# A chunk scan of a state-space branch: from a doubling scan on two engines to a tree on one, with 128-row output matmuls

## The chip, the cores and the metric

The kernel runs on one core of one Trainium2 chip. The metric is the device time of one execution in microseconds (us). Several executions are made and their median is taken.

## What is computed

Two transformer-like blocks run one after the other on 1024 tokens of width 1024, all in float32. The first holds attention, a state-space (SSM) branch and a convolutional feed-forward; the second holds three gated branches. Only the SSM branch is touched by the change. The reference computes it as a scan over tokens:

```python
def combine(left, right):
    ar1, ai1, xr1, xi1 = left
    ar2, ai2, xr2, xi2 = right
    return (ar2 * ar1 - ai2 * ai1,
            ar2 * ai1 + ai2 * ar1,
            ar2 * xr1 - ai2 * xi1 + xr2,
            ar2 * xi1 + ai2 * xr1 + xi2)

_, _, xr, xi = lax.associative_scan(combine, (a_re_t, a_im_t, bu_re, bu_im), axis=1)
y = (jnp.einsum('bsgn,gcn->bsgc', xr, c_re)
     - jnp.einsum('bsgn,gcn->bsgc', xi, c_im) + d_skip * ug)
```

There are 16 groups of 64 complex states; `a` does not depend on the token.

## The kernel before

All the large products are TensorE matmuls whose operands are split into a high and a low part (`fp32r`), three matmuls for one product. A weight block of 128x1024 comes in by DMA, ScalarE casts its high part and VectorE subtracts to get the low part (`split_to`, lines 608 to 626; this is called a split below). A matmul cannot start before its block is split.

The order of the work is not written by hand. Every operation is recorded in a `Plan` (line 155); `schedule` (lines 293 to 444) plays the recorded program with a cost for each operation and with a limit on the live buffers (`NSLOT` = 50 of 128x1024, kinds of them with limits of their own), and `issue` hands the instructions to the engines in the order that results. So every instruction has the line 450, each engine works off its own fixed list, and a list waits as a whole when its next instruction waits. Buffers have the names `s…`, PSUM tiles `mm…` (two banks) and `tr…` (one bank).

The SSM branch is a generator, `ssm_gen` (line 964). The code that computes the attention and SSM gates (lines 1557 to 1569) takes up to `NSTEP` = 3 steps of it after each gate block. A gate block is one weight block and 48 matmuls of 512 columns in one `mm` tile, and the gate blocks are the work that TensorE has beside the scan. The tokens are cut into 128 chunks of 8. `vr` and `vi` (line 1211) hold for each chunk the state that it adds, real and imaginary part, 128 partitions (two halves of 64 states) by 8 groups by 128 chunks. Lines 1227 to 1247 scan over the 128 chunks in seven doubling levels; at level `l` every chunk from `d = 2**l` on gets a rotated copy of the chunk `d` before it:

```python
pt(q[2], v3r[:, :, 0:w], ai, ALU.mult)      # GpSimd
pt(q[3], v3i[:, :, 0:w], ar, ALU.mult)      # GpSimd
tt(q[0], v3r[:, :, 0:w], ar, ALU.mult)      # VectorE, as the four below
tt(q[1], v3i[:, :, 0:w], ai, ALU.mult)
tt(q[0], q[0], q[1], ALU.subtract)
tt(v3r[:, :, d:], v3r[:, :, d:], q[0], ALU.add)
tt(q[2], q[2], q[3], ALU.add)
tt(v3i[:, :, d:], v3i[:, :, d:], q[2], ALU.add)
```

This is 42 operations on VectorE and 14 on GpSimd. Then (lines 1249 to 1265) 16 groups give their output in one PSUM tile for every four: a matmul of `ut` with `kt` on 128 rows, and one each of `vr` with `car` and of `vi` with `cai` on the 64 rows of the group's half. These are 48 plain float32 matmuls of 128 columns; the profile counts two records for each. They are called the output matmuls below. A gelu follows (`gelu2`, on ScalarE and VectorE), transposes, and a small gated product. The kernel then goes on to the query and key blocks and the attention.

Of the kernel before, what the change touches and what calls it, by code (L numbers as in the profile page):

```python
# [14 lines left out]
AF = mybir.ActivationFunctionType  # L15
ALU = mybir.AluOpType
# [449 lines left out]
def kernel(ctx: ExitStack, tc: tile.TileContext, x, wts, wada, vecs, rows, ssmv, wglu, ttab, iden,  # L466
                           out, dbg=None):
    nc = Plan(tc.nc)
# [15 lines left out]
    def slot(p, dt=F32, group=None):  # L484
        return nc.buffer(dt, group)
# [56 lines left out]
    def mm(ps, l, r, start, stop):  # L542
        nc.tensor.matmul(out=ps, lhsT=l, rhs=r, start=start, stop=stop)

    def act(o, i, f, scale=1.0, bias=0.0, acc=None):
        kw = {}
        if acc is not None:
            kw["accum_out"] = acc
        nc.scalar.activation(out=o, in_=i, func=f, scale=scale, bias=bias, **kw)
# [4 lines left out]
    def tt(o, a, b, op):  # L554
        nc.vector.tensor_tensor(out=o, in0=a, in1=b, op=op)

    def ts(o, a, s1, s2, op0, op1=None):
        if op1 is None:
            nc.vector.tensor_scalar(out=o, in0=a, scalar1=s1, scalar2=None, op0=op0)
        else:  # L560
            nc.vector.tensor_scalar(out=o, in0=a, scalar1=s1, scalar2=s2, op0=op0, op1=op1)
# [402 lines left out]
    def ssm_gen(xs):  # L964
# [83 lines left out]
        z = mul(r, r)  # L1048
        sp = lin(z, -1.9515295891e-4, 8.3321608736e-3)
        sp = mul(sp, z)  # L1050
        q = T()
# [173 lines left out]
            yield  # L1225

        v3r, v3i = (v.rearrange("p (a j) -> p a j", a=8) for v in (vr, vi))
        for l in range(7):
            d = 1 << l
            w = 128 - d  # L1230
            ar = pre(8 + l).rearrange("p (a o) -> p a o", o=1).to_broadcast([128, 8, w])
            ai = pim(8 + l).rearrange("p (a o) -> p a o", o=1).to_broadcast([128, 8, w])
            q = [slot("t").rearrange("p (a j) -> p a j", a=8)[:, :, 0:w] for _ in range(4)]

            def pt(o, x_, y_, op):
                nc.gpsimd.tensor_tensor(out=o, in0=x_, in1=y_, op=op)

            pt(q[2], v3r[:, :, 0:w], ai, ALU.mult)
            pt(q[3], v3i[:, :, 0:w], ar, ALU.mult)
            tt(q[0], v3r[:, :, 0:w], ar, ALU.mult)  # L1240
            tt(q[1], v3i[:, :, 0:w], ai, ALU.mult)
            tt(q[0], q[0], q[1], ALU.subtract)
            yield
            tt(v3r[:, :, d:], v3r[:, :, d:], q[0], ALU.add)
            tt(q[2], q[2], q[3], ALU.add)
            tt(v3i[:, :, d:], v3i[:, :, d:], q[2], ALU.add)
            yield

        yg = [slot("yg"), slot("yg")]
        for gh in range(2):  # L1250
            k3 = kt[gh].rearrange("p (t g c) -> p t g c", t=8, g=8)
            y3 = yg[gh].rearrange("p (t c) -> p t c", t=8)
            for h in range(2):
                ps = tr_ps()
                p3 = ps.rearrange("p (t g c) -> p t g c", t=8, g=4)
                for j in range(4):
                    gl = 4 * h + j
                    pr, b = gl, 64 * gh
                    o = p3[:, :, j, :]
                    mm(o, ut[gh][:, 128 * gl:128 * gl + 128], k3[:, :, gl, :], True, False)  # L1260
                    mm(o, vr[b:b + 64, 128 * pr:128 * pr + 128], car[b:b + 64, 128 * pr:128 * pr + 128], False, False)
                    mm(o, vi[b:b + 64, 128 * pr:128 * pr + 128], cai[b:b + 64, 128 * pr:128 * pr + 128], False, True)
                t = slot("gl")
                gelu2(y3[:, :, 64 * h:64 * h + 64], ps, t, lambda a: a.rearrange("p (t c) -> p t c", t=8))
                yield
# [1134 lines left out]
```

## Time and profile before

| | us |
|---|---|
| median of three runs | 2127.89 |
| the runs | 2118.71, 2127.90, 2127.89 |
| the profiled execution, its own time | 2118.8 |
| its span, first to last instruction | 2116.7 |
| TensorE (PE) busy in it | 2032.1 (96%) |
| VectorE (DVE) busy | 1375.1 (65%) |
| ScalarE (ACT) busy | 748.4 (35%) |
| GpSimd (POOL) busy | 494.9 (23%) |
| mean granted TensorE clock | 0.977 of full speed |

A row of the profile gives engine, operation, output and inputs by name (numbers left out), shape, count and duration. `idle before <-` names what ended an idle time. A count of PE is in records: a `fp32r` matmul of 512 columns is one, a plain float32 matmul two.

### The profile page before, as it was taken

What the parts mean: (1) busy time and instruction counts of PE and PEld (TensorE: products, weight loads), DVE (VectorE), ACT (ScalarE), POOL (GpSimd) and SP (SyncE); (2) the same over time, 40 slices, a digit from 0 to 9 for tenths busy, and PEclk for the clock granted to TensorE, in tenths of its full rate; (3) what the DMA queues carried; (4) which work ended last, traced back from release to release, by engine and by line L of the source; (5) the groups of instructions that cost most, each with busy time, mean ns of one, the idle gap of its engine ahead of it and who ended that gap; (6) DMA issues with size and microseconds to landing.
All of it is one profiled execution on the core that took longest, in us unless ns stands there. A gap on an engine that the chain in (4) does not pass through costs nothing. (4 is left out here: it accounts for less than half of the span.)

```text
span 2116.7 us, 24506 instructions
## 1 busy us (share of the span) xinstructions
PE 2032.1 (96%) x9366; PEld 1675.6 (79%) x9366; DVE 1375.1 (65%) x2147; ACT 748.4 (35%) x1153; POOL 494.9 (23%) x436
## 2 busy tenths in 40 slices
PE   5999889999999999999999997999999999989998
PEld 3788778888888788888888875888888888867887
DVE  8768885787673862544447588687878755573645
ACT  4412215767421433122212264343433434361212
POOL 5201531222202100000003247422423333211320
PEclk7999999999999999999999997999999999999999
DMA  8336334431742321212121231401421332163312
GB/s 331 119 143 228 112 121 126 103 97 53 290 153 80 116 99 40 71 40 70 50 90 61 75 126 44 169 11 60 169 87 64 129 111 108 50 268 139 115 55 80
DMA packets 71317, 235.55 MB, mean 111 GB/s; under 512 B 8224, under 2 KB 12672, under 8 KB 71200
## 3 DMA queue, kind: packets, MB, share of 16 engines
q1 hardware_dynamic: 46368, 157.88, 21.1%
q0 software_dynamic: 24832, 76.10, 10.6%
q8 instruction: 74, 1.21, 0.2%
q14 instruction: 43, 0.35, 0.1%
HBM read 177.79 MB, written 47.19 MB: 106 GB/s over the span
## 5 line engine op out<-in xcount | busy, mean ns | idle before, releaser
L450 PE MATMUL mm<-s,s 128*128 128x512 f32 x5000 | 1184.7, 394 | 33.7 <-DVE s L450 27.5
L450 PEld LDWEIGHTS mm<-s,s 128*128 128x128 f32 x5000 | 944.4, 190 | 238.3 <-DVE s L450 32.7
L450 PE MATMUL tr<-s,s 128*128 128x512 f32 (+3 forms) x3696 | 823.1, 378 | 16.3 <-DVE s L450 12.2
L450 PEld LDWEIGHTS tr<-s,s 128*128 128x128 f32 (+2 forms) x3696 | 650.7, 189 | 146.7 <-DVE s L450 18.7
L450 DVE TENSOR_TENSOR s<-s,s 128x512 fp32r<-128x512 f32 (+10 forms) x569 | 580.2, 1048 | 120.2 <-ACT s L450 64.2
L450 ACT CAST s<-s 128x512 fp32r<-128x512 f32 (+3 forms) x420 | 304.7, 747 | 432.6 <-PE mm L450 185.7
L450 POOL TENSOR_TENSOR s<-s,s 128x512 f32<-128x512 f32 (+9 forms) x166 | 284.4, 1719 | 497.9 <-ACT s L450 231.5
L450 ACT ACTIVATE s<-s 128x1024 f32<-128x1024 f32 (+3 forms) x171 | 161.3, 945 | 427.7 <-DVE s L450 331.8
L450 DVE TENSOR_TENSOR s<-s,mm 128x512 f32<-128x512 f32 (+1 forms) x138 | 101.9, 739 | 127.2 <-PE mm L450 126.4
L450 DVE SCALAR_TENSOR_TENSOR s<-s,s 128x1024 fp32r<-128x1024 f32 (+2 forms) x81 | 101.9, 1263 | 94.9 <-ACT s L450 94.8
L450 ACT COPY s<-tr 128x512 f32<-128x512 f32 (+2 forms) x146 | 76.6, 532 | 148.0 <-PE tr L450 129.4
L450 POOL TENSOR_TENSOR s<-s 128x512 f32<-128x512 f32 x60 | 88.8, 1482 | 128.2 <-DMA s<-in_wts_dram 74.0
L450 DVE TENSOR_TENSOR s<-s,tr 128x512 f32<-128x512 f32 (+1 forms) x152 | 93.4, 627 | 31.3 <-PE tr L450 26.5
L450 ACT ACTIVATE s<-s,sm 128x512 f32<-128x512 f32 (+7 forms) x119 | 90.4, 774 | 54.0 <-DVE sm L450 53.2
L450 PE MATMUL tr<-idn,s 128*128 128x128 f32 x608 | 92.0, 283 | 16.1 <-ACT s L450 11.4
L450 DVE TENSOR_TENSOR s<-tr,s 128x512 fp32r<-128x512 f32 (+3 forms) x97 | 61.9, 650 | 62.0 <-PE tr L450 43.6
L450 PEld LDWEIGHTS tr<-idn,s 128*128 128x128 f32 x608 | 74.7, 146 | 34.6 <-ACT s L450 15.0
L450 DVE SCALAR_TENSOR_TENSOR s<-mm,vt,s 128x1023 f32<-128x1023 f32 (+3 forms) x36 | 41.8, 1162 | 87.3 <-ACT s L450 86.9
L450 DVE SCALAR_TENSOR_TENSOR s<-s,mm 128x1024 f32<-128x1024 f32 x40 | 48.8, 1219 | 59.6 <-PE mm L450 56.6
L450 ACT ACTIVATE s<-mm,hb 128x1024 f32<-128x1024 f32 x15 | 16.7, 1116 | 112.7 <-PE mm L450 103.8
L450 POOL DMA_DIRECT2D gt_d<-s x2 | 1.1, 534 | 232.3 <-DVE s L450 232.3
L450 POOL DMA_DIRECT2D s<-s x48 | 25.5, 538 | 85.3 <-ACT s L450 65.6
(106 smaller groups left out, 669.1 us busy)
## 6 DMA issues: line engine op xcount, KB each, us to landing
s<-in_wts_dram SPq DMA_DIRECT2D x172, 512.0 KB, 4.0
s<-in_wada_dram SPq DMA_DIRECT2D x48, 512.0 KB, 6.6
g_d<-s POOLq DMA_DIRECT2D x24, 512.0 KB, 2.9
s<-g_d SPq DMA_DIRECT2D x24, 512.0 KB, 8.0
s<-s POOLq DMA_DIRECT2D x32, 256.0 KB, 4.4
s<-in_x_dram SPq DMA_DIRECT2D x8, 512.0 KB, 9.0
v_d<-s POOLq DMA_DIRECT2D x8, 512.0 KB, 7.8
gs_d<-s POOLq DMA_DIRECT2D x8, 512.0 KB, 3.9
```

The costliest lines, as they stand in the source:

```text
L450: hook(getattr(getattr(self.nc, eng), method)(*args, **kw), self.ops[i][7] + f"|{self.start[i]:.0f}|{i}")
```

## The change

The doubling scan becomes a scan up and down a tree. On the way up, level `l` (0 to 6) updates one chunk in every `2d`, so 64, 32, … 1 chunks; on the way down (levels 5 to 0) it fills in 1, 3, 7, … 63 chunks. Real and imaginary parts stand side by side in one operation: each step has two products of 16·w elements per partition (w the number of chunks), one sum of 16·w, and two additions of 8·w into `vr` and `vi`, all on VectorE. The chunks of a step lie `2d` elements apart in `vr` and `vi`. A small table `rot` is made by 14 operations of 8 elements; it stands in the free part of the buffer `pd`. GpSimd has no part in the scan any more. The scan has 11 steps of the generator where it had 14.

The output matmuls of `vr` and `vi` work on all 128 rows; ScalarE makes copies `cz` of `car` and `cai`, four buffers of 128x1024, in which the half that doesn't belong to the group is multiplied by zero.

```diff
--- before.py
+++ after.py
@@ -1225,26 +1225,44 @@
             yield
 
         v3r, v3i = (v.rearrange("p (a j) -> p a j", a=8) for v in (vr, vi))
+        rot = pd[:, 256:256 + 16 * 7]
         for l in range(7):
+            ts(rot[:, 16 * l:16 * l + 8], pim(8 + l), -1.0, None, ALU.mult)
+            nc.vector.tensor_copy(out=rot[:, 16 * l + 8:16 * l + 16], in_=pre(8 + l))
+
+        def step(l, down):
             d = 1 << l
-            w = 128 - d
-            ar = pre(8 + l).rearrange("p (a o) -> p a o", o=1).to_broadcast([128, 8, w])
-            ai = pim(8 + l).rearrange("p (a o) -> p a o", o=1).to_broadcast([128, 8, w])
-            q = [slot("t").rearrange("p (a j) -> p a j", a=8)[:, :, 0:w] for _ in range(4)]
-
-            def pt(o, x_, y_, op):
-                nc.gpsimd.tensor_tensor(out=o, in0=x_, in1=y_, op=op)
-
-            pt(q[2], v3r[:, :, 0:w], ai, ALU.mult)
-            pt(q[3], v3i[:, :, 0:w], ar, ALU.mult)
-            tt(q[0], v3r[:, :, 0:w], ar, ALU.mult)
-            tt(q[1], v3i[:, :, 0:w], ai, ALU.mult)
-            tt(q[0], q[0], q[1], ALU.subtract)
+            n = 64 // d
+            w = n - 1 if down else n
+
+            def at(v, m, i0):
+                return v.rearrange("p a (i m) -> p a i m", m=2 * d)[:, :, i0:i0 + w, m]
+
+            src, dst, i0 = (2 * d - 1, d - 1, 1) if down else (d - 1, 2 * d - 1, 0)
+            two = lambda a: a.rearrange("p (h a o) -> p h a o", h=2, o=1).to_broadcast([128, 2, 8, w])
+            one = lambda a: a.rearrange("p (h a) w -> p h a w", h=1).to_broadcast([128, 2, 8, w])
+            q = [slot("t")[:, 0:16 * w].rearrange("p (h a i) -> p h a i", h=2, a=8) for _ in range(2)]
+            tt(q[0], one(at(v3r, src, 0)), two(pw[:, 16 * (8 + l):16 * (9 + l)]), ALU.mult)
+            tt(q[1], one(at(v3i, src, 0)), two(rot[:, 16 * l:16 * l + 16]), ALU.mult)
+            tt(q[0], q[0], q[1], ALU.add)
+            for h, v in enumerate((v3r, v3i)):
+                o = at(v, dst, i0)
+                tt(o, o, q[0][:, h], ALU.add)
+
+        for l in range(7):
+            step(l, False)
             yield
-            tt(v3r[:, :, d:], v3r[:, :, d:], q[0], ALU.add)
-            tt(q[2], q[2], q[3], ALU.add)
-            tt(v3i[:, :, d:], v3i[:, :, d:], q[2], ALU.add)
-            yield
+        for l in range(5, -1, -1):
+            step(l, True)
+            if l % 2:
+                yield
+        yield
+        cz = []
+        for s__ in (car, cai):
+            z = [slot("cz") for _ in range(2)]
+            for i in range(2):
+                act(z[i], s__, AF.Identity, scale=half[:, i:i + 1])
+            cz.append(z)
 
         yg = [slot("yg"), slot("yg")]
         for gh in range(2):
@@ -1255,11 +1273,12 @@
                 p3 = ps.rearrange("p (t g c) -> p t g c", t=8, g=4)
                 for j in range(4):
                     gl = 4 * h + j
-                    pr, b = gl, 64 * gh
+                    pr = gl
                     o = p3[:, :, j, :]
                     mm(o, ut[gh][:, 128 * gl:128 * gl + 128], k3[:, :, gl, :], True, False)
-                    mm(o, vr[b:b + 64, 128 * pr:128 * pr + 128], car[b:b + 64, 128 * pr:128 * pr + 128], False, False)
-                    mm(o, vi[b:b + 64, 128 * pr:128 * pr + 128], cai[b:b + 64, 128 * pr:128 * pr + 128], False, True)
+                    c_ = slice(128 * pr, 128 * pr + 128)
+                    mm(o, vr[:, c_], cz[0][gh][:, c_], False, False)
+                    mm(o, vi[:, c_], cz[1][gh][:, c_], False, True)
                 t = slot("gl")
                 gelu2(y3[:, :, 64 * h:64 * h + 64], ps, t, lambda a: a.rearrange("p (t c) -> p t c", t=8))
                 yield
```

Here is what the schedule makes of it at three places. The first is VectorE where the scan begins; `s_1307` is `vr`, `s_1315` is `vi`, `s_1279` the powers of `a`, `s_2569` the buffer with `rot`, and an operation that writes 128x1024 from two other buffers (`s_3120`, `s_3035`) is the low part of a split. Before:

```order
L450 TENSOR_TENSOR mod<-mod,vt 128x8
L450 TENSOR_TENSOR s_3061<-s_1307,s_1279 128x8x127
L450 TENSOR_TENSOR s_3074<-s_1315,s_1279 128x8x127
L450 TENSOR_TENSOR s_3061<-s_3061,s_3074 128x8x127
L450 TENSOR_TENSOR s_1307<-s_1307,s_3061 128x8x127
L450 TENSOR_TENSOR s_2770<-s_2770,s_3049 128x8x127
L450 TENSOR_TENSOR s_1315<-s_1315,s_2770 128x8x127
L450 TENSOR_TENSOR s_3120<-s_2937,s_2979 128x1024
```

and now:

```order
L450 TENSOR_TENSOR mod<-mod,vt 128x8
L450 TENSOR_TENSOR s_3035<-s_2939,s_3003 128x1024
L450 TENSOR_TENSOR s_3045<-s_1307,s_1279 128x1024
L450 TENSOR_TENSOR s_3058<-s_1315,s_2569 128x1024
L450 TENSOR_TENSOR s_3045<-s_3045,s_3058 128x1024
L450 TENSOR_TENSOR s_1307<-s_1307,s_3045 128x512
L450 TENSOR_TENSOR s_1315<-s_1315,s_3045 128x512
L450 TENSOR_TENSOR s_3083<-s_1307,s_1279 128x512
L450 TENSOR_TENSOR s_3088<-s_1315,s_2569 128x512
L450 TENSOR_TENSOR s_3083<-s_3083,s_3088 128x512
L450 TENSOR_TENSOR s_1307<-s_1307,s_3083 128x256
L450 TENSOR_TENSOR s_1315<-s_1315,s_3083 128x256
```

What moved: the six operations of a level make way for the five of a step with shrinking sizes, and the next split (`s_3106`) comes behind two steps.

The second is TensorE where the output matmuls begin (`tr_402` to `tr_407`; the names after the arrow are the moving and the stationary operand, `s_2711` is `car`, `s_2773` the half-zero copy of it). Before:

```order
L450 MATMUL mm_406<-s_1648,s_3081 128x512 x2
L450 MATMUL mm_406<-s_1661,s_3081 128x512 x2
L450 MATMUL mm_406<-s_1648,s_3360 128x512
L450 MATMUL tr_403<-s_2711,s_1307 128x8x16
L450 MATMUL tr_404<-s_2711,s_1307 128x8x16
L450 MATMUL tr_405<-s_2711,s_1307 128x8x16
L450 MATMUL mm_406<-s_1648,s_3360 128x512
L450 MATMUL mm_406<-s_1686,s_3081 128x512 x2
L450 MATMUL mm_406<-s_1697,s_3081 128x512 x2
```

and now:

```order
L450 MATMUL mm_405<-s_1545,s_3049 128x512 x2
L450 MATMUL mm_405<-s_1552,s_3049 128x512 x2
L450 MATMUL mm_405<-s_1545,s_3226 128x512
L450 MATMUL tr_402<-s_2773,s_1307 128x8x16
L450 MATMUL tr_403<-s_2773,s_1307 128x8x16
L450 MATMUL tr_404<-s_2783,s_1307 128x8x16
L450 MATMUL tr_402<-s_2793,s_1315 128x8x16
L450 MATMUL tr_402<-s_1335,s_2615 128x8x16
```

What moved: the output matmuls stood 23 records into `mm_406`, the sixth gate block counted from `mm_398`, and stand now 17 records into `mm_405`, the fifth.

The third is TensorE ahead of the scan, where the state matmuls (`tr_397`) end and gate block `mm_398` begins (`s_1335` is `kt`, `tr_387` and `tr_388` are sums over partitions for the modulation, which the VectorE stretch with the scan is queued behind). Before:

```order
L450 MATMUL tr_397<-s_2615,s_2669 64x128
L450 MATMUL tr_397<-s_2629,s_2669 64x128
L450 MATMUL mm_398<-s_1458,s_2895 128x512 x2
L450 MATMUL mm_398<-s_1468,s_2895 128x512 x2
L450 MATMUL mm_398<-s_1458,s_2913 128x512 x2
```

and now:

```order
L450 MATMUL tr_397<-s_2615,s_2669 64x128
L450 MATMUL tr_397<-s_2629,s_2669 64x128
L450 MATMUL tr_402<-s_1335,s_2615 128x8x16
L450 MATMUL tr_403<-s_1335,s_2615 128x8x16
L450 MATMUL mm_398<-s_1458,s_2983 128x512 x2
L450 MATMUL mm_398<-s_1468,s_2983 128x512
L450 MATMUL tr_387<-s_2998,onesr 128x512
L450 MATMUL tr_388<-s_2998,onesr 128x512
L450 MATMUL mm_398<-s_1468,s_2983 128x512
L450 MATMUL mm_398<-s_1458,s_2996 128x512 x2
```

What moved: the first matmuls with `kt` and the modulation's sums stand at the beginning of `mm_398` instead of at its end.

## Rows read from the trace of the kernel before

**Rows 1.** Busy time of each engine by stretch, around and after the scan

```profile
core 0: us, PE busy (x) PEld busy (x) DVE busy (x) ACT busy (x) POOL busy (x), PEclk, DMA share, GB/s
250.00:300.00 50.00, 39.62 (x154) 30.75 (x152) 49.26 (x37) 6.25 (x6) 25.11 (x15) 0.86 0.33 107
300.00:350.00 50.00, 50.00 (x247) 40.76 (x248) 24.34 (x29) 18.32 (x23) 7.70 (x14) 1.00 0.44 134
```

**Rows 2.** Timeline of PE: start, us, operation, count, idle before and releaser

```profile
230.36 22.08 PE L450 MATMUL mm<-s,s 128*128 128x512 f32 x96
...
252.41 1.18 PE L450 MATMUL mm<-s,s 128*128 128x512 f32 x4
258.65 13.59 PE L450 MATMUL mm<-s,s 128*128 128x512 f32 x48 [5.06 <-DVE s L450]
274.51 11.18 PE L450 MATMUL mm<-s,s 128*128 128x512 f32 x48 [2.27 <-DVE s L450]
288.74 7.31 PE L450 MATMUL mm<-s,s 128*128 128x512 f32 x19 [3.05 <-DVE s L450]
295.99 0.71 PE L450 MATMUL tr<-s,s 64*128 64x128 f32 x6
```

**Rows 3.** Timeline of DVE, the stretch that holds the scan

```profile
232.03 67.81 DVE L450 TENSOR_TENSOR s<-s,s 128x1016 f32<-128x1016 f32 x49
```

**Rows 4.** Busy time by stretches of 5 us, columns as in rows 1

```profile
260.00:265.00 5.00, 5.00 (x15) 3.92 (x15) 4.96 (x4) 0.00 (x0) 3.87 (x2) 0.62 0.00 0
275.00:280.00 5.00, 5.00 (x24) 4.12 (x23) 4.86 (x4) 0.00 (x0) 1.00 (x1) 1.00 0.06 21
290.00:295.00 5.00, 5.00 (x14) 3.86 (x14) 4.90 (x6) 0.00 (x0) 4.11 (x4) 0.54 0.00 0
```

**Rows 5.** Groups by shape, DVE, 232 to 300 us: count, busy us, mean ns

```profile
L450 DVE TENSOR_TENSOR s<-s,s 128x1008 f32<-128x1008 f32 x6 | 10.3, 1738 | 0.2
...
L450 DVE TENSOR_TENSOR s<-s,s 128x1024 fp32r<-128x1024 f32 x6 | 7.2, 1216 | 0.0
L450 DVE TENSOR_TENSOR s<-s,s 128x512 f32<-128x512 f32 x6 | 4.8, 827 | 0.1
L450 DVE TENSOR_TENSOR s<-s,s 128x512 fp32r<-128x512 f32 x1 | 0.7, 683 | 0.0
```

**Rows 6.** Groups by shape, whole span: small operations of DVE

```profile
L450 DVE TENSOR_TENSOR s<-s,s 128x128 f32<-128x128 f32 x32 | 8.2, 311 | 0.0
...
L450 DVE TENSOR_TENSOR sm<-s 128x8 f32<-128x8 f32 x54 | 7.0, 161 | 0.0
```

**Rows 7.** Groups by shape: the copy at 108 to 130 us, and at 316 to 326 us

```profile
L450 DVE COPY s<-tr 128x512 f32<-128x512 f32 x4 | 2.6, 686 | 7.2 <-PE tr L450 7.2
...
L450 DVE COPY s<-tr 128x512 f32<-128x512 f32 x4 | 4.3, 1168 | 0.0
```

**Rows 8.** Busy time by stretch: plain float32 matmuls, output, small and transposes

```profile
298.43:308.58 10.15, 10.15 (x61) 7.86 (x60) 6.42 (x9) 1.77 (x3) 0.00 (x0) 1.00 0.61 193
...
189.71:193.60 3.89, 3.89 (x35) 3.68 (x33) 3.85 (x3) 1.39 (x2) 3.15 (x2) 1.00 0.94 319
172.36:174.20 1.84, 1.84 (x17) 1.66 (x15) 1.81 (x2) 1.68 (x4) 0.34 (x1) 1.00 0.58 220
```

**Rows 9.** Timeline of PE, then of ACT, from the state matmuls on

```profile
215.78 1.31 PE L450 MATMUL tr<-s,s 128*64 128x128 f32 x20
217.02 9.82 PE L450 MATMUL mm<-s,s 128*128 128x512 f32 x42
...
217.36 1.06 ACT L450 CAST s<-s 128x1024 fp32r<-128x1024 f32 x1
...
218.78 2.02 ACT L450 CAST s<-s 128x1024 fp32r<-128x1024 f32 x2
```

**Rows 10.** Timeline of POOL, and DMA issues (KB, us to landing), for `kt`

```profile
211.25 4.69 POOL L450 DMA_DIRECT2D s<-s  x9 [4.34 <-DVE s L450]
...
s<-s POOLq DMA_DIRECT2D x2, 64.0 KB, 3.2
```

**Rows 11.** Timeline of DVE and PE around 200 us, the modulation's sums

```profile
197.92 1.23 DVE L450 TENSOR_TENSOR s<-s,s 128x1024 fp32r<-128x1024 f32 x1 [1.16 <-ACT s L450]
...
199.44 0.62 PE L450 MATMUL tr<-s,onesr 128*128 128x512 f32 x2
```

## The prediction

> **What bounds the kernel now.** I read the table by engine first: PE is busy for 96% of the span, so the kernel is as long as its matmuls plus what PE loses. Then the busy time by stretches: the reader is to see that PE loses 10.4 us between 250 and 300 us, where DVE is busy for 49.3 of 50 us and the granted clock is 0.86, and nothing in the next 50 us, where DVE is half idle [rows 1]. Then PE's timeline there: three gate blocks in a row wait for DVE, 5.06, 2.27 and 3.05 us [rows 2]. DVE is in one unbroken run of 49 operations and 67.81 us [rows 3]: the 42 of the scan and 7 splits, for which PE waits. The splits are short, 6 x 1216 ns + 683 ns = 8.0 us, so the scan is 59.8 us [rows 5]. A scan operation of 1008 elements takes 1738 ns there where a split of 1024 takes 1216 [rows 5]; GpSimd works on the scan at the same time. Last I read the clock after two of the waits: in 5 us PE gets through 15 and 14 records where it gets through 24 at the full clock [rows 4]. The mean granted clock of 0.62 and 0.54 says that most of those stretches ran at the lower level, 1.2 of 2.4 GHz, after PE had stood still.
>
> So the loss in this stage is known from PE's own rows. From 252.41 to 295.99 us it worked off 4 + 48 + 48 + 19 = 119 records of 512 columns, just ahead it took 22.08 / 96 = 0.230 us for one [rows 2]. 119 x 0.230 = 27.4 of 43.6 us: **16.2 us are lost**, 10.4 in waits and 5.8 at the lower clock.
>
> **The scan.** Over the 13 steps the widths add up to 127 on the way up and 120 on the way down. A step of width w handles 3 x 16w + 2 x 8w = 64w elements, together 15,808 in 65 operations; the old scan handled some 36,900 on DVE in 42. DVE takes 161 ns for 8 elements, 311 for 128, 683 for 512 and 1216 for 1024 [rows 5, 6], which is close to 0.16 us + 1.03 ns per element: 65 x 0.16 + 16.3 = 26.7 us. That holds for neighbouring elements. The tree's lie 2d apart in `vr` and `vi`, and the trace shows one operation both ways: the copy of 512 elements takes 686 ns when it writes runs of 16, and 1168 when each element goes 32 bytes on [rows 7]. That is 0.94 ns more per element. In a step the two products and the two additions touch such operands, 48w elements; over all steps 11,856, at 0.94 ns 11.1 us more, without the two widest steps (stride 8 bytes) 5,760 elements and 5.4 us. So the tree costs between 26.7 and 37.9 us; I take 32.1, since no row shows a stride of 8 bytes to be dear, and one shows 32 bytes to be. The Trainium skill (SBUF — State Buffer, Door 1: The DMA port swizzle) has a rule against this change: SBUF is read in lines of 16 bytes, and an access that goes to a new line each time pays, while two hits in a line don't; by it, too, the widest steps would be free and all others dear, though it gives no price.
>
> Does PE still wait? Count from the moment at which PE has done the second pair of modulation sums (`tr_388`) early in `mm_398`. Ahead of the output matmuls PE then has 41 records of `mm_398`, 3 x 48 and 17, that is 202 x 0.230 = 46.5 us. DVE has the two products and the sum for the modulation and a split, 3.9 us by its durations for such sizes, then the tree with three splits inside (3.7 us): 3.9 + 32.1 + 3.7 = 39.7 us, 6.8 ahead of PE; with the dearest tree 45.5, still ahead. The splits inside come behind the second, sixth and eighth step, each well before its block's turn on PE. So no wait of this stage is left, and with none the clock stays up: **-16.2 us**. The next to be late would be the gelu behind the outputs; DVE is half idle there [rows 1], and the 31 records left of `mm_405` (7.1 us) and the last outputs cover its chain.
>
> **The output matmuls.** 96 records now take 0.168 us each (60 in 10.15) [rows 8]. Two of every six use 128 rows and four use 64. Plain float32 records that all use 128 rows take 1.84 / 16 = 0.115 us (transposes, 128 columns) and 3.89 / 33 = 0.118 (32 columns) [rows 8]. With a zeroed half all use 128. At 0.118 the 96 take 11.3 instead of 16.1 us: **-4.8 us**. The bounds are 0 (still 0.168) and -5.1 (0.115) on one side, and on the other the 0.230 of a full 512 columns, +6.0. I take 0.118, which is the same kind of matmul. Two rules of the Trainium skill speak here. TensorEngine Tiling (Key Properties) says that a change of the tiling mode drains TensorE; by it the mix of 64 and 128 rows costs and the gain is the one taken. TensorE: Matmul & The Clock Gate (LDWEIGHTS, loading the stationary operand) says that the load of the stationary operand depends on its columns and not on its rows; by that alone nothing changes, and the sum would be 4.8 us poorer. The rows favour the first.
>
> **What is added ahead of the scan.** Four ScalarE operations for `cz` and the 14 for `rot` fall where both engines have room, but they shift the order, and four more buffers of the 50 are held until the outputs. Three things come earlier on PE's list than their inputs may be ready. (1) The modulation's second pair near 199.4 us: nine small operations (9 x 0.2 us) come ahead of the split that feeds it, which had 1.16 us of idle time before it [rows 11], and the pair comes some 1.6 us sooner: about 0.5 us of wait. (2) `tr_402` needs the eighth DMA for `kt`, issued some 7 x 0.53 us after 211.25 and landing 3.2 us on, at 218.2 us, when PE would come to it at 217.0 [rows 9, 10]. (3) `mm_398` now needs a cast that ScalarE does behind the copy of the state matmuls, at 217.36 to 218.42, and the first modulation sum the cast at 218.78 to 219.8 [rows 9]. (2) and (3) overlap; PE would start at 218.5 instead of 217.0 and wait once more for 0.7: 2.2 us. Together **+2.7 us**, between 0 and, with one spell at the lower clock (2.9 us, half of the 5.8), 5.6.
>
> GpSimd's 14 operations leave, with nothing waiting for them but the scan. The rest of the program keeps its order from some 600 us on; in the attention before that it is shuffled a little, under PE that hardly waits, and I cost that at nothing. If its cover went, it would show as PE waits between 320 and 600 us.
>
> **Sum.** -16.2 - 4.8 + 2.7 = -18.3 us. From the profiled execution's own 2118.8 us that gives 2100.5. This execution lies with the lowest run; the median of 2127.89 lies 9.1 higher, with two of the three. One trace can't tell what the higher level consists of, and of four known executions two lie on each. I put the median in the middle, 4.5 above: **2105 us**.
>
> **The rivals.** Half a per cent, 10.6 us, is about what a measurement of this kernel can tell from no change.
>
> Rival 1, **the outputs stay at 0.168**: the 0.168 comes from the strided reads of `kt`, not from the 64 rows. For it: every third pair of records has them. Against: the uniform rows at 0.115 and 0.118. Then 2105 + 4.8 = 2109.8 us. It is also what follows from the rule of TensorE: Matmul & The Clock Gate above.
>
> Rival 2, **PE waits for weights instead of VectorE**: four held buffers let fewer weight blocks be prepared ahead, and not only `mm_398` but each of the next three blocks waits for its cast. Price 4 x 2.2 us and a spell at the lower clock, 11.7 where I have 2.7: 2105 + 9 = 2114 us, not to be told from before by the lower level. For it: the cast for `mm_398` has already moved behind other work. Against: the later casts stand far ahead on ScalarE's list, and ScalarE works 6 of 50 us there [rows 1].
>
> Rival 3, **the time is given back in the attention** by its shuffled order: about 2118 us. Against: PE is at 50.00 of 50 us in the first stretch of it [rows 1].
>
> Rival 4, **slower: the tree is too dear.** If strided operands cost far more than the copy shows, or each of 65 dependent operations waits for the one before, PE stands before the output matmuls. The tree may take 46.5 - 7.6 = 38.9 us without harm; at X us it costs X - 38.9 and 2.9 for the clock, so the kernel is slower from X = 54 (twice the plain cost), and measurably from 65. At three times, 80 us, it is 2105 + 41 + 3 = 2149 us. Against: the copy shows at most 1.7 times, and dependent operations of the old scan ran without gaps [rows 3].
>
> **How the numbers follow.** The forecast has a chance of 0.58, rival 1 0.20, rival 2 0.12, rival 3 0.04, rival 4 0.06. The low end is the forecast without the new waits (2102) and, since the median may fall on the lower level or the far side of the unknown costs, 10 below that; the high end takes in rivals 1 and 2 with the rest of the higher level: 2092 to 2117. Faster: forecast and rival 1, 0.78; within half a per cent: rivals 2 and 3, 0.16; slower: rival 4, 0.06.
>
> **What would show it.** In the changed profile DVE should have a stretch of some 40 us with operations of 1024 down to 8 elements and no operations of 1008, and PE no wait for DVE longer than 1 us up to the output matmuls, with the clock at 1.00. The 128-row output records should stand near 0.12 us. Around 217 to 220 us PE should wait some 2 us, for a DMA or ScalarE. The forecast is wrong if PE stands for more than 3 us before the output matmuls, or if their records stay at 0.168, or if losses of more than 5 us turn up between 320 and 600 us.

## The result, and the profile after

The changed kernel takes **2097.19 us** (median of four runs, 2095.84 to 2099.59). The kernel before took 2123.57 beside it (four runs, 2118.71 to 2127.90). The ratio is 0.9868, with an interval of 0.9845 to 0.9891: 1.3% faster. The profiled execution of the changed kernel took 2095.84 us with a span of 2094.0, so it is 23 us under the profiled one of before.

Between 250 and 300 us, where PE lost most of its time, it now loses none. The busy time by stretches [rows 1], for the changed kernel (columns as there):

```profile
core 0: us, PE busy (x) PEld busy (x) DVE busy (x) ACT busy (x) POOL busy (x), PEclk, DMA share, GB/s
216.00:228.00 12.00, 10.34 (x48) 8.66 (x49) 9.49 (x10) 8.03 (x9) 3.45 (x7) 1.00 0.35 113
228.00:250.00 22.00, 22.00 (x99) 18.23 (x98) 15.36 (x42) 4.35 (x4) 1.07 (x2) 1.00 0.42 144
250.00:300.00 50.00, 50.00 (x277) 43.29 (x275) 32.42 (x48) 16.56 (x20) 3.65 (x6) 1.00 0.41 132
```

PE is busy for all of 250 to 300 us at the full clock, where it had 39.6 us at 0.86. One loss is left ahead of it, between 216 and 228 us. PE's timeline of the changed kernel shows which (start, us, operation, count, idle before and releaser) [rows 2, 9]:

```profile
213.78 1.31 PE L450 MATMUL tr<-s,s 128*64 128x128 f32 x20
217.66 0.68 PE L450 MATMUL tr<-s,s 128*128 128x128 f32 x4 [2.56 <-DMA s<-s]
218.10 0.94 PE L450 MATMUL mm<-s,s 128*128 128x512 f32 x3
...
220.72 42.10 PE L450 MATMUL mm<-s,s 128*128 128x512 f32 x185
...
266.78 7.53 PE L450 MATMUL tr<-s,s 128*128 128x128 f32 x66
274.06 7.32 PE L450 MATMUL mm<-s,s 128*128 128x512 f32 x31
281.23 2.84 PE L450 MATMUL tr<-s,s 128*128 128x128 f32 x24
```

After the state matmuls PE waits 2.56 us for a `kt` DMA. From there to the outputs it doesn't wait once. The outputs are the 66 and 24 records; the 66 start within 274.06 - 266.78 = 7.28 us, 0.110 for one, where it was 0.168 [rows 8].

DVE's timeline of the changed kernel in place of its 67.81 us [rows 3]:

```profile
223.36 16.96 DVE L450 TENSOR_TENSOR s<-s,s 128x1024 fp32r<-128x1024 f32 x29
240.64 3.34 DVE L450 TENSOR_TENSOR s<-s,s 128x32 f32<-128x32 f32 x15 [0.32 <-PE mm L450]
246.71 0.24 DVE L450 TENSOR_TENSOR s<-s,s 128x48 f32<-128x48 f32 x1 [2.73 <-DMA ga_d<-s]
251.52 16.39 DVE L450 TENSOR_TENSOR s<-s,s 128x48 f32<-128x48 f32 x27 [4.56 <-PE mm L450]
```

and its groups by shape, from 223 to 269 us (count, busy us, mean ns, idle before) [rows 5, 6]:

```profile
L450 DVE TENSOR_TENSOR s<-s,s 128x1024 fp32r<-128x1024 f32 x7 | 8.4, 1219 | 0.0
...
L450 DVE TENSOR_TENSOR s<-s,s 128x1024 f32<-128x1024 f32 x3 | 3.6, 1219 | 0.0
L450 DVE TENSOR_TENSOR s<-s,s 128x1008 f32<-128x1008 f32 x3 | 3.5, 1205 | 0.0
...
L450 DVE TENSOR_TENSOR s<-s,s 128x496 f32<-128x496 f32 x3 | 2.7, 924 | 0.0
...
L450 DVE TENSOR_TENSOR s<-s,s 128x504 f32<-128x504 f32 x2 | 1.3, 680 | 0.0
```

The seven operations of the first row are splits. The 65 operations of the tree fill some 28.5 us (the busy times of their groups together), where the 42 of the doubling scan filled 59.8. The tree stands still twice for longer than 1 us, for 2.73 and 4.56 us. Both times the next operation is a product of 48 elements and by the releaser its temporary buffer was not yet free: the one was being stored to `ga_d`, the other was being read by PE. The tree's last operation ends at 264.5 us, 2.3 us ahead of the outputs; three splits come behind it.

**How the stage is measured below.** Single executions also differ outside the stage that is changed: the first of four small transposes (`tr<-idn`, near 186 us), ahead of all that the change touches, starts between 185.5 and 187.9 us in five profiles of the unchanged kernel. So I compare kernels by the time from that transpose to the first store into `h_d`. For the changed kernel the two rows are these, in the views of the two tiles (shortest, median and longest ns; first and last start; form):

```profile
L450 PE MATMUL tr<-idn,s x4: 271/272/273, 185.5 to 185.8; 128*128 128x128 f32 x4
L450 POOL DMA_DIRECT2D h_d<-s x16: 540/540/617, 610.8 to 696.4; - x16
```

610.8 - 185.5 = 425.3 us. Worked out in the same way for every profile of this study:

| profile | stage, us | time of the profiled execution, us |
|---|---|---|
| before | 445.8 | 2118.8 |
| before, further profiles (the runs b2, b3, b5) | 446.1, 445.5, 445.4 | 2119.5, 2116.4, 2116.3 |
| before, a run of the upper level (b4) | 455.9 | 2128.3 |
| changed | 425.3 | 2095.8 |
| changed, again (a2) | 425.6 | 2096.1 |
| E1: tree, outputs on 64 rows | 428.4 | 2099.9 |
| E2: doubling scan, outputs on 128 rows | 442.8 | 2116.4 |
| E3: doubling scan, all on VectorE | 440.0 | 2112.4 |
| E4: tree, one product on GpSimd | 428.5 | 2101.0 |
| E5: changed, `kt` matmul last | 424.4 | 2097.3 |
| E6: changed, `cz` made later | 423.0 | 2094.8 |

The change takes 20.5 us out of the stage. Of the 22.7 us between the two spans another 1.9 are the earlier start, which is chance (b3 and b5, unchanged, start at 185.6 and 185.5 too).

### The profile page after: what moved, and what is told of

Read it like the earlier page. It is cut to its first block, busy times and chain, and to the rows that moved or that the text cites. A ratio compares the mean times of both kernels' runs of the same rounds, so it can differ in the third digit from the quotient of the medians.

```text
span 2094.0 us, 24517 instructions
## 1 busy us (share of the span) xinstructions
PE 2017.2 (96%) x9366; PEld 1668.4 (80%) x9366; DVE 1344.6 (64%) x2184; ACT 752.7 (36%) x1157; POOL 461.5 (22%) x422
## 5 line engine op out<-in xcount | busy, mean ns | idle before, releaser
L450 PEld LDWEIGHTS mm<-s,s 128*128 128x128 f32 x5000 | 939.1, 189 | 225.7 <-DVE s L450 20.8
L450 PEld LDWEIGHTS tr<-s,s 128*128 128x128 f32 (+1 forms) x3696 | 648.4, 188 | 145.5 <-DVE s L450 18.0
L450 DVE TENSOR_TENSOR s<-s,s 128x512 fp32r<-128x512 f32 (+11 forms) x592 | 548.0, 955 | 130.9 <-ACT s L450 66.0
L450 ACT CAST s<-s 128x512 fp32r<-128x512 f32 (+4 forms) x420 | 304.6, 748 | 437.4 <-PE mm L450 178.6
L450 POOL TENSOR_TENSOR s<-s,s 128x512 f32<-128x512 f32 (+5 forms) x152 | 250.3, 1653 | 457.2 <-ACT s L450 233.2
L450 ACT ACTIVATE s<-s,sm 128x256 f32<-128x256 f32 (+7 forms) x119 | 90.3, 774 | 58.1 <-DVE sm L450 57.5
L450 DVE SCALAR_TENSOR_TENSOR s<-s,mm 128x1024 f32<-128x1024 f32 x40 | 48.7, 1219 | 59.7 <-PE mm L450 59.7
L450 ACT ACTIVATE s<-mm,vt 128x1024 f32<-128x1024 f32 (+1 forms) x18 | 20.0, 1110 | 66.3 <-PE mm L450 65.7
```

Source lines behind the costliest of these rows:

```text
L450: hook(getattr(getattr(self.nc, eng), method)(*args, **kw), self.ops[i][7] + f"|{self.start[i]:.0f}|{i}")
```

## The experiments

**E1: the tree alone.** The changed kernel without `cz`; the output matmuls of `vr` and `vi` work on 64 rows as before.

```diff
-        cz = []
...
-                    mm(o, vr[:, c_], cz[0][gh][:, c_], False, False)
-                    mm(o, vi[:, c_], cz[1][gh][:, c_], False, True)
...
+                    mm(o, vr[b:b + 64, c_], car[b:b + 64, c_], False, False)
+                    mm(o, vi[b:b + 64, c_], cai[b:b + 64, c_], False, True)
```

> The tree alone: outputs as before, on 64 rows, no zeroed copies. If the tree is what takes PE's waits away and the 128-row outputs are worth some 5 us by themselves (theory): no PE wait for DVE over 1 us up to the outputs, output records near 0.168 us instead of 0.111, the wait of 2.6 us for the kt transfers gone, since four buffers fewer are held and mm_398 has its weights in time; in all 2 to 4 us slower than the change, 2098 to 2101 us. If the rows don't matter (rival 1 of the prediction, the strided reads of kt): records the same in both, near 0.11, and the kernel 2 us faster than the change. If the outputs carry most of the gain: above 2110 us.

2101.08 us (four runs, 2099.91 to 2101.72; ratio to before 0.9893, 0.9853 to 0.9932). PE's timeline of E1:

```profile
214.53 1.31 PE L450 MATMUL tr<-s,s 128*64 128x128 f32 x20
215.78 8.69 PE L450 MATMUL mm<-s,s 128*128 128x512 f32 x37
...
228.29 32.94 PE L450 MATMUL mm<-s,s 128*128 128x512 f32 x144
261.15 10.66 PE L450 MATMUL tr<-s,s 64*128 64x128 f32 x66
```

and DVE's:

```profile
229.88 33.15 DVE L450 TENSOR_TENSOR s<-s,s 128x1024 f32<-128x1024 f32 x69
```

PE waits for nothing, not even for `kt`: the first gate block follows the state matmuls at once. The tree runs unbroken, 65 operations and 4 splits in 33.15 us, which leaves 28.3 for the tree. So the tree by itself is worth 445.8 - 428.4 = 17.4 us. The outputs stay near what they were, 10.60 / 66 = 0.161 us a record. Here is the busy time over the two stretches of outputs, E1 and then the changed kernel (columns as above):

```profile
261.15:271.75 10.60, 10.60 (x68) 8.30 (x67) 6.09 (x8) 2.83 (x4) 2.06 (x3) 1.00 0.74 238
282.76:286.88 4.12, 4.12 (x25) 3.15 (x23) 1.23 (x1) 1.11 (x1) 0.55 (x1) 1.00 0.32 124
```

```profile
266.78:274.06 7.28, 7.28 (x67) 7.28 (x66) 3.77 (x6) 2.65 (x4) 0.00 (x0) 1.00 0.84 262
281.23:283.90 2.67, 2.67 (x25) 2.67 (x24) 1.22 (x1) 1.11 (x1) 0.53 (x1) 1.00 0.03 6
```

The 90 records take 14.72 us in E1 and 9.95 in the changed kernel. The single records of E1's trace show where the time goes. In the first stretch the rows change 18 times between 64 and 128; the first record after each change starts 0.20 us after the one before it and the second 0.21 us after the first. Nearly all other records, those on 64 rows too, stand 0.11 us apart, as the changed kernel's do.

**E2: the outputs alone.** The kernel before with `cz` and 128-row outputs.

```diff
+            for i in range(2):
+                act(z[i], s__, AF.Identity, scale=half[:, i:i + 1])
...
-                    mm(o, vr[b:b + 64, 128 * pr:128 * pr + 128], car[b:b + 64, 128 * pr:128 * pr + 128], False, False)
...
+                    mm(o, vr[:, c_], cz[0][gh][:, c_], False, False)
...
```

> The outputs alone: the old doubling scan with the zeroed copies and 128-row outputs. Theory: the three waits of PE for DVE (10 us together) and the spells at the lower clock stay, the output records go to 0.11 us (-5 us), and a wait for kt or weights of 2 us comes, since the copies hold four buffers: some 3 us faster than before, 2115 to 2121 us with before's own spread. If the outputs carry most of the gain: under 2106 us, with the waits shrunk.

2111.67 us (ten runs, 2109.21 to 2116.41; ratio 0.9945, 0.9926 to 0.9964), faster than the 2115 to 2121 expected. PE's timeline of E2:

```profile
221.53 1.19 PE L450 MATMUL tr<-s,s 128*128 128x128 f32 x4 [3.59 <-DMA s<-s]
...
271.94 11.20 PE L450 MATMUL mm<-s,s 128*128 128x512 f32 x48 [1.09 <-DVE s L450]
286.17 9.07 PE L450 MATMUL mm<-s,s 128*128 128x512 f32 x26 [3.04 <-DVE s L450]
...
297.38 6.86 PE L450 MATMUL tr<-s,s 128*128 128x128 f32 x60
```

The records come down to 0.11 us with the old scan too, and the strided reads of `kt` are still there. So it is the rows that count, not `kt` and not the tree, and by E1's single records it is the change of rows, not the 64 rows themselves. The wait for `kt` is there as well, 3.59 us: it belongs to `cz`.

What E2 is worth in time isn't settled. Its stage is 3.0 us shorter, but this execution is the slowest of the ten, 7.2 us over the fastest, and no other one has a profile. So that E1's 17.4 and E2's 3.0 come near the change's 20.5 doesn't show that the two parts are independent. E2 also changes more than the outputs: with `cz` the schedule lets the scan begin 41.9 us after the first small transpose instead of 44.7, and two waits for VectorE, of 1.09 and 3.04 us, are left where three of 10 us together were expected to stay. Beside the tree the outputs on 128 rows are worth 428.4 - 425.3 = 3.1 us: 4.8 less for the outputs and 2.6 more for the `kt` wait; the other 0.9 us are not placed.

**E3: GpSimd's part.** The doubling scan as before, with its two GpSimd products for each level on VectorE.

```diff
             def pt(o, x_, y_, op):
-                nc.gpsimd.tensor_tensor(out=o, in0=x_, in1=y_, op=op)
+                nc.vector.tensor_tensor(out=o, in0=x_, in1=y_, op=op)
```

> The old doubling scan with its 14 GpSimd products moved to VectorE, outputs as before. Theory: VectorE's operations were stretched by GpSimd's work on the same buffers (1738 ns for 1008 elements against 1216 for 1024), so that the help was worth next to nothing: 56 operations at 0.16 us + 1.03 ns per element are 59.7 us, against 59.8 us for 42; the time is that of before within 4 us, and the operations of 1008 elements take 1.2 us. If GpSimd's share really relieved VectorE: 14 us more of VectorE, as much more of PE waits, 2130 to 2140 us.

2112.62 us (ten runs, 2111.36 to 2114.62; ratio 0.9950, 0.9931 to 0.9970), faster than expected. DVE's timeline of E3, then two of its groups by shape in that stretch:

```profile
230.44 63.84 DVE L450 TENSOR_TENSOR s<-s,s 128x1016 f32<-128x1016 f32 x62
```

```profile
L450 DVE TENSOR_TENSOR s<-s,s 128x1008 f32<-128x1008 f32 x8 | 9.3, 1204 | 0.1
...
L450 DVE TENSOR_TENSOR s<-s,s 128x512 f32<-128x512 f32 x8 | 5.2, 686 | 0.1
```

Without its 6 splits (7.2 us) and the short one (0.7) this is 55.9 us for 55 operations; with the one that stands ahead of the stretch (1.2) it is 57.1 for 56, where 42 had taken 59.8. The same operation of 1008 elements takes 1204 ns alone and 1738 beside GpSimd [rows 5]. At E3's mean the 42 would take 42 / 56 x 57.1 = 42.8 us, so GpSimd's 14 products cost VectorE 17.0 us, and VectorE does them itself in 14.3. **The second engine was worth less than nothing**, 2.7 us. The Trainium skill (SBUF — State Buffer, Who interferes with whom) says that an operation of VectorE with two inputs in SBUF and one of GpSimd that reads SBUF hold a shared port one at a time. The runs agree with it as far as VectorE goes, whose operations got longer; they don't show whether GpSimd's did too. The stage is 5.8 us shorter, which is more than these 2.7: the scan also begins 43.2 us after the first small transpose instead of 44.7, and one operation stands ahead of it.

**E4: GpSimd in the tree.** The changed kernel with the second product of each step on GpSimd; one run.

```diff
-            tt(q[1], one(at(v3i, src, 0)), two(rot[:, 16 * l:16 * l + 16]), ALU.mult)
+            nc.gpsimd.tensor_tensor(out=q[1], in0=one(at(v3i, src, 0)), in1=two(rot[:, 16 * l:16 * l + 16]), op=ALU.mult)
```

> The tree with one of its two products per step on GpSimd. Theory: what must be short now is the chain of 13 dependent steps up to the outputs, not VectorE's busy time; a product of 1024 elements takes GpSimd some 2.7 us, so the chain grows by some 10 us while VectorE does less; it ended 2.5 us ahead of PE in the change, so PE waits 3 to 8 us before the outputs and the kernel is 3 to 12 us slower than the change. If VectorE's busy time is what counts: not slower than the change.

2100.96 us, which lies in the expected range, but not for the expected reason: the wait ahead of the outputs did not come. PE's timeline of E4:

```profile
219.56 1.20 PE L450 MATMUL tr<-s,s 128*128 128x128 f32 x4 [2.98 <-DMA s<-s]
...
225.84 41.68 PE L450 MATMUL mm<-s,s 128*128 128x512 f32 x183
...
272.39 7.53 PE L450 MATMUL tr<-s,s 128*128 128x128 f32 x66
```

and the busy time of E4 behind that wait (columns as above):

```profile
219.50:225.80 6.30, 6.24 (x17) 5.16 (x18) 0.47 (x1) 4.10 (x5) 3.21 (x4) 0.52 0.53 194
```

The tree ends at 271.5 us instead of at 264.5, 0.9 us ahead of the outputs. It starts 5 us later than in the changed kernel, of which 1.5 are the later start of the stage, and from the first operation of its stretch to its last it takes 43.1 us instead of 41.1. The schedule puts more records of the gate blocks ahead of the outputs, and PE comes to them just in time. The stage is 3.2 us longer, and that is all at the `kt` wait: the wait is 0.4 longer, and the clock behind it is 0.52. The four records of `kt` take 0.85 us instead of 0.44, and the 13 from 220.41 to 225.84 take 0.42 each where the changed kernel's 11 take 0.24 (218.10 to 220.72), 13 x 0.18 = 2.3 us; together 3.1. So GpSimd's part in the tree stretched the chain, and in this one run it cost nothing by itself. The place where E4 lost its time is the `kt` wait. The same might happen to the changed kernel, whose runs reach 2101.68 us, but neither of its two profiles shows it.

**E5 and E6: where the wait for `kt` comes from.** The orders of the programs differ in one point: with `cz` (changed kernel, E2, E4) two `kt` matmuls stand ahead of the first gate block, without it (before, E1) they don't. Either the late DMA costs the time, or the four buffers that `cz` takes early: the block's weights are then prepared late and the recorded program is scheduled around them. E5 takes the `kt` matmuls out of the way; E6 gives the buffers back for a while.

```diff
E5
-                    mm(o, ut[gh][:, 128 * gl:128 * gl + 128], k3[:, :, gl, :], True, False)
...
+                    mm(o, ut[gh][:, c_], k3[:, :, gl, :], False, True)
E6
         for l in range(7):
             step(l, False)
+            at_ = len(nc.ops) - 1
             yield
...
+                nc.after = (at_,)
                 act(z[i], s__, AF.Identity, scale=half[:, i:i + 1])
+                nc.after = ()
```

> The changed kernel with one thing moved: in each group of the output matmuls the product of ut with kt comes last instead of first, so that it is not put ahead of the first gate block's matmuls (mm_398). If the 2.56 us that TensorE stood still at 217.66 us in the changed kernel came from the late kt DMA standing at the head of its list, TensorE is at mm_398 at once and waits at most 1.0 us there for ScalarE's cast; the stage up to the output matmuls gets 1.5 to 2.5 us shorter and the time is 1.5 to 2.5 us under the changed kernel's in the same set (2095 us where that has 2097). If the DMA is only the one that shows and mm_398's weights come just as late, TensorE waits 2 us or more at the same place for ScalarE or VectorE and the time is the same within 0.7 us.

> The changed kernel with the four cz copies held back until the last step of the way up the tree, by a dependence in the recorded program; nothing else is changed. If the four buffers that cz holds early are why the first gate block's weights are prepared late (and with them the kt matmuls come ahead of mm_398 and wait for their DMA), mm_398 now follows the state matmuls without a wait, no wait over 0.5 us is left between 215 and 225 us, and the time is 2 to 3 us under the changed kernel's in the same set (2094.5 where that has 2097). The outputs stay at 0.111 us for a record. If the buffers have no part in it, the wait of about 2.5 us at 217 us is still there and the time is the same within 0.7 us.

> The changed kernel once more, beside the two kernels above on the same chip. Expected is its time again, 2097 us within 2, with the 2.6 us wait for the kt DMA near 217 us, outputs at 0.111 us a record, and a start of the state-space branch's first small transposes between 187.8 and 189.8 us. If the 1.9 us by which its profile was ahead of the profile of before at 188 us was chance and not the change, this profile may show either.

In that set the changed kernel took 2098.11 us (2096.07 to 2101.68), E5 2097.41 (2096.70 to 2098.69) and E6 **2095.04** (2094.32 to 2096.68), four runs each. PE's timeline of E5, then of E6:

```profile
217.20 0.97 PE L450 MATMUL mm<-s,s 128*128 128x512 f32 x3 [0.75 <-ACT s L450]
218.63 0.73 PE L450 MATMUL tr<-s,onesr 128*128 128x512 f32 x2 [0.46 <-ACT s L450]
```

```profile
215.46 1.31 PE L450 MATMUL tr<-s,s 128*64 128x128 f32 x20
216.70 8.69 PE L450 MATMUL mm<-s,s 128*128 128x512 f32 x37
```

In E5 1.21 us of waits for ScalarE's casts are left of the 2.56 to 2.80 for the DMA; the stage is 0.9 to 1.2 us shorter, and the median not measurably. So neither of the two expectations came: the DMA was half of that wait and late weights the other half. In E6 no wait is left, and the stage is 2.3 to 2.6 us shorter, as expected of the buffers. ScalarE's time for the copies is not the cause: in the changed kernel it made them between 188 and 196 us and stood idle before the casts for `mm_398`, as its timeline shows:

```profile
214.27 0.58 ACT L450 COPY s<-tr 128x508 f32<-128x508 f32 x1 [10.14 <-PE tr L450]
```

That it is the buffers, and not only the other order of the program, is argued: E6 moves the copies together with their buffers, and no run held the buffers without the copies. E6 is the fastest kernel of the study, by its median 2 to 3 us under the changed kernel; its slowest run lies among the changed kernel's faster ones.

**The two levels of the kernel before.** Its runs fall on 2116 to 2120 or 2127 to 2129 us, in one set 9 and 10 of 19. No tree kernel here had two such levels, in 21 runs. Four more profiles of the kernel before, with no edit, were to catch the upper one:

> The kernel before once more, for a profile. Its runs lie on two levels, about 2118 and 2128 us. If this profile is one of 2128, the 9 us between them should be found in one place: either more time at the lower clock in the scan stage (250 to 300 us), after the waits of 5.06, 2.27 and 3.05 us, or elsewhere. If they are in the scan stage, the change removes them with the waits, and the measured gain is larger than the gain between the two profiles by about half of them. If they are elsewhere (before 190 us or after 600 us), the higher level has nothing to do with the scan, and its absence from the changed kernel is a side effect of the shift in time or of chance.

> The kernel before, for one more profile: two so far are of its lower level (2118.8 and 2119.5 us), none of the higher (2126.8 to 2129.1). If this one is of the higher level, one theory looks for its 9 us in the scan stage, as more time at the lower clock between 240 and 300 us; then the change removes them together with the waits. The rival looks for them outside it (before 190 or after 320 us), where the change alters nothing.

> As the run before this one: a further profile of the kernel before, to catch one of its higher level. Theory: the 9 us are a longer spell at the lower clock between 240 and 300 us. Rival: they lie before 190 or after 320 us.

> As the two runs before this one: a further profile of the kernel before, to catch one of its higher level. Theory: the 9 us are a longer spell at the lower clock between 240 and 300 us. Rival: they lie before 190 or after 320 us.

b2, b3 and b5 are of the lower level (2119.51, 2116.41, 2116.25 us), b4 of the upper (2128.32). PE's timeline of b5 at the end of the scan, then that of b4:

```profile
286.92 6.22 PE L450 MATMUL mm<-s,s 128*128 128x512 f32 x19 [3.07 <-DVE s L450]
293.87 0.71 PE L450 MATMUL tr<-s,s 64*128 64x128 f32 x6 [0.73 <-DVE s L450]
294.51 1.89 PE L450 MATMUL mm<-s,s 128*128 128x512 f32 x7
296.33 10.22 PE L450 MATMUL tr<-s,s 64*128 64x128 f32 x60
306.47 4.38 PE L450 MATMUL mm<-s,s 128*128 128x512 f32 x18
```

```profile
288.36 4.64 PE L450 MATMUL mm<-s,s 128*128 128x512 f32 x19 [3.02 <-DVE s L450]
295.32 0.71 PE L450 MATMUL tr<-s,s 64*128 64x128 f32 x6 [2.32 <-DVE s L450]
295.96 2.44 PE L450 MATMUL mm<-s,s 128*128 128x512 f32 x7
298.33 18.08 PE L450 MATMUL tr<-s,s 64*128 64x128 f32 x60
316.34 6.52 PE L450 MATMUL mm<-s,s 128*128 128x512 f32 x18
```

VectorE does the same in both, 49 operations in 67.80 us. In b5 part of the 19 records behind the third wait runs at the lower clock (6.22 us). In b4 they run at the full one (4.64), PE reaches the outputs sooner and waits 2.32 us for the last scan operations instead of 0.73, and now the outputs run at the lower clock: 60 records in 18.08 us instead of 10.22, and the 18 behind them in 6.52 instead of 4.38. In steps of 5 us, b4 (columns as above):

```profile
290.00:295.00 5.00, 3.00 (x14) 2.13 (x12) 4.90 (x6) 0.00 (x0) 3.91 (x4) 1.00 0.04 6
295.00:300.00 5.00, 4.68 (x18) 3.19 (x19) 4.43 (x6) 0.00 (x0) 0.00 (x0) 0.71 1.24 348
300.00:305.00 5.00, 5.00 (x18) 3.97 (x18) 0.00 (x0) 0.22 (x1) 0.00 (x0) 0.50 0.44 171
```

The clock is 0.50, the level of 1.2 GHz, from here to 320 us. The 10 us between the levels are in the stage (455.9 against 445.8 us), as the theory had it, though most of them lie behind its 300 us. They are not the wait itself: measured from the first small transpose the 60 records start after 111.4 us in b4 and after 110.9 in b5. From there on the 60 and the 18 records take 24.6 us instead of 14.6, and those are the 10 us. So in this one profile of the upper level they are the price of the lower clock behind a fourth wait for the scan. Why the clock stays up behind the third wait in b4 and not in the others, these runs don't show.

## Why the prediction was right, point by point

The forecast was 2105 us, in a range of 2092 to 2117; 2097.19 came. The forecast for the profiled execution was 2100.5; 2095.84 came. The range was wide, in part because the two levels were not understood, so that the time lies in it says little by itself; the terms say more.

- **The waits and the lower clock, -16.2.** Right. The tree alone gives 17.4 (E1). 0.55 of the difference is the short wait that ends at 230.12 us, which the working did not count and which is gone too.
- **The tree, 32.1 us between 26.7 and 37.9.** Right, a little dear. The durations of its 65 operations add up to 31.0 us; they overlap at their ends, so that together they fill 28.5. The price of stride: products of 1024 and 1008 elements with a stride of 8 bytes cost what the sums of neighbouring elements in the same rows do, 1219 and 1205 ns in the mean. The 496 elements take 924 ns in the mean of two products with a stride of 16 bytes and a sum without, where 504 with 8 bytes take 680. Singly the products take 1046 ns and the sum 679, 0.74 ns more per element, where 0.94 was taken from the copy. So the choice of which steps are dear was right. The rule of the Trainium skill (SBUF — State Buffer, Door 1: The DMA port swizzle), that an access to a new 16-byte line pays and two hits in a line don't, agrees with these rows. One sign of the forecast was wrong by its own numbers: operations of 1008 elements had to be there, since the last step down has 16 x 63 of them in an operation.
- **The slack of 6.8 us ahead of PE.** Wrong in its size. 2.3 us were left, with a shorter tree: it stood still for 7.3 us, by the releasers because temporary buffers were still in use. "The splits inside" were looked at, the buffers of the products were not. E1, with four buffers more to spare, has no such gap. It cost nothing here, but it shows how near the changed kernel is to a wait.
- **The outputs, -4.8, at 0.118.** Right: 0.110 came, and from E1 to the changed kernel the records take 14.72 - 9.95 = 4.8 us less. That the sum is met so closely is in part luck: a record became cheaper than forecast, and fewer than 96 stood in the mix of rows. In the changed kernel the weight loads fill the stretch of the outputs wholly (7.28 of 7.28 us), in E1 8.30 of 10.60, with the same duration for a load of 64 and of 128 rows (186 and 188 ns in E1). So the loads were not dearer; there were gaps between them where 64 and 128 rows took turns. A rule of the Trainium skill fits that (TensorEngine Tiling (Array Packing), Key Properties): a change of tiling mode drains TensorE.
- **The added waits, +2.7.** The sum was right, 2.56 came. Of its two terms the `kt` wait came (2.2 forecast), and the 0.5 us at the modulation's pair did not: the small operations there start every 0.07 us, not every 0.2. The cause was half seen: late casts and the late DMA were both named, but it is the early `cz` copies, with the four buffers that they hold, that bring both about (E6).
- **Nothing given back in the attention.** Right: the gain of 20.5 us at `h_d` is the gain at the end (22.7 - 1.9 = 20.8 us) within 0.3 us.
- **The middle of the two levels, +4.5.** This is the term that missed: "One trace can't tell what the higher level consists of", and the forecast carried half of it over into the changed kernel. In b4, the one profile of the upper level, its 10 us stand behind a wait for the scan, which the change removes. Without the 4.5 the forecast is 2100.5; the stage's 2.2 us more and the start's 1.9 lead to 2096.4, beside 2095.84 measured for that execution. It is also why the medians differ by 26 us and the profiles by 23.

Rival 1 (outputs stay at 0.168) fell with E2. Rival 2 (held buffers) fits E6 in its cause and was far too dear: one wait, not four. Rivals 3 and 4 did not show.

## What to carry to other kernels

When a second engine helps with a chain of element-wise operations, price the chain with it and without it from the durations of the same shape alone and beside the other: here the help of 14 operations cost 17.0 us to save 14.3. A wait of TensorE is priced with the lower clock that follows it, and if runs of a kernel lie on two levels, look first whether such a spell lands on different work in each. And what a change holds early, here four buffers, has to be looked for in the waits of its neighbours: taken later, they left no wait.

## What the runs showed that was not expected

- 14 operations of GpSimd made 42 operations of VectorE take 59.8 us instead of some 42.8; one of 1008 elements took 1738 ns beside GpSimd and 1204 alone.
- A matmul record of the outputs took 0.30 us at the lower clock (60 in 18.08), 0.170 at the full one with 64 and 128 rows mixed (60 in 10.22), and 0.110 with 128 rows throughout. In the mix only the two records after a change of rows stand 0.20 to 0.21 us behind the one before, the others 0.11.
- A last wait of PE that was 1.6 us longer went with a kernel that was 10 us longer, by where the lower clock fell behind it.
- Small operations of VectorE that don't need one another overlap: those of 8 elements for `rot` take 0.16 us each and start every 0.07 us (nine of them from 193.01 to 193.75 us).
